# An MoE after three dense layers on one Trainium2 core: tokens gathered from three bf16 parts instead of fp32, expert biases from two fp32r matmuls instead of four fp32

## The chip, the cores and the metric

One of the eight cores of one Trainium2 chip. The metric is the device time of one execution in microseconds, the median of several runs.

## The reference

Two blocks follow each other on 256 tokens of width 1024, all in fp32. The first block has two layers: an RG-LRU mixer and a forgetting attention, each followed by a squared-ReLU MLP. The second has a mixer of stick-breaking attention and an HGRN2 recurrence with gates, then LayerNorm and a mixture of 32 experts, of which each token takes four. The change lies in the mixture:

```
logits = xt @ router_w + router_b
top_vals, top_idx = top_k(logits, 4);  gates = softmax(top_vals)
# for each expert e, on the tokens xblk that chose it:
hcat = xblk @ w_up[e] + b_up[e]                     # 1024 -> 2048
x_glu = min(hcat[:, 0::2], 7);  x_lin = clip(hcat[:, 1::2], -7, 7)
act = x_glu * sigmoid(1.702 * x_glu) * (x_lin + 1)  # 1024
y = act @ w_down[e] + b_down[e]                     # 1024 -> 1024
out = sum over the four experts of gate * y
# then layer_norm(2**0.25 * h + out)
```

## The kernel before

**Dense part (to about 825 us).** Dense weights come in pieces of 1 MiB into the five sections of `area`; ScalarE rounds each half to fp32r (`wh`, line 407), VectorE subtracts the rest (`wl`, line 385), and three fp32r matmuls (lines 487 to 489) make the product. The last one, with `w_out_2`, ends in `residual` for two halves of the tokens and of the columns. Its LayerNorm's statistics come from `bn_stats`; `cross` turns x into `xs` for the router's `logits` (line 1587), `best` and `chosen` find each token's four experts as ones in `M`, and the matmuls `prk` (1654 to 1656) number the tokens of each expert. The order of all instructions is written by hand: each engine runs its own in the order of the code.

**Experts.** A loop goes over 32 positions. `rank_experts` sorts the experts by their load, apart from the first two, so that expert number and column of a position come from the selector `Q`. A position works on one unit of 64 token slots, position 12 on two. For each unit:

- `P` (`spread`, line 1611): 256 tokens x 64 slots of ones and zeros on VectorE, from the position's column. `gather` (1677) multiplies the normed tokens with it on TensorE, line 1685, 8 blocks of 128 columns x 2 halves of the tokens, and VectorE applies the norm's gain and bias (1691, 1692): `xT`, the unit's tokens with columns on the partitions. Columns are taken at every second place, since the weights lie with two rows on one partition.
- `first_layer` (1710): `first_bias` (1547) starts both PSUM banks `hp` with the bias row of the expert: the bias is spread over 4 x 32 partitions in `bup`, and the selector column picks the row. Then 8 weight chunks of 1 MiB with 4 fp32 matmuls each (line 1719); the outputs for gate and linear columns lie in the two halves of the PSUM partitions.
- `gated` (lines 1733 to 1743) on VectorE and ScalarE, while TensorE turns the gates (`pG`, 1704) and gathers the next position's tokens; then TensorE turns the result (`turned`, `paT`, 1761), and ScalarE copies it to `aT`.
- `second_layer`: 4 chunks, 4 fp32 matmuls each (1783); `keep` splits y in two fp32r parts; `combine` (1805, 1806) scatters them into x during the next position.

A matmul of fp32 leaves two records in the trace, of fp32r or bf16 one.

**Weights.** 32 experts x 12 chunks x 1 MiB = 384 MiB come through SyncE's queue into 20 slots of 1 MiB, most in pairs of 2 MiB (`load_chunk`, issued on line 324). `release(j)` after chunk j's last matmul issues the next load into the slots that came free; the functions that `later` names for a place run there too: in position 0 `rank_experts`, `gates_of_tokens`, `number_experts`, `by_token` (which fills `RGT`), `by_position` (`RP`), `residual_sum`, and in position 3 `list_overflow`. The first 20 chunks are loaded during the last dense products, each as soon as a pool closes.

Of the kernel before, what the change touches and what calls it, by code (L numbers as in the profile page):

```python
# [21 lines left out]
KT = 8  # L22
# [56 lines left out]
def shape_constants():  # L79
# [19 lines left out]
    block = i[:, None] // NE == np.arange(4)  # L99
    f["block"] = block  # L100
    f["first"] = (block[:, :, None] & (i[:, None, None] % NE == np.arange(2))).reshape(128, 8)
# [23 lines left out]
def fused(ctx: ExitStack, tc: tile.TileContext, d, out, dbg=None):  # L125
# [1071 lines left out]
    with ExitStack() as mixo, ExitStack() as attn:  # L1197
# [283 lines left out]
        fill((8, rawD))  # L1481
        route_b = mo.tile([128, 2, 128], BF, name="route_b")
# [45 lines left out]
        out_proj(w, [(i, i) for i in range(4)], True)  # L1528
        w = row_weights(d["w_out_2"][0], 512, 512)
# [25 lines left out]
        first_b = C("first").rearrange("p (b e) -> p b e", b=4)  # L1555
        nx = mo.tile([128, 2, D], F32, name="nx")
        xs = [nx[:, t].rearrange("p (k t) -> p k t", k=KT) for t in range(2)]
# [71 lines left out]
        rawF = ctx.enter_context(tc.tile_pool(name="rawF", bufs=1, side="right", reuse_waits="tile"))  # L1629
        fill((14, rawC), (17, rawF))  # L1630
# [20 lines left out]
        early_hps = [[[bank("hp") for _ in range(2)]] for _ in range(2)]  # L1651
        first_bias(early_hps[0], first_b[:, :, 0:1])
# [16 lines left out]
    Q = ml.tile([128, 4, NE], F32, name="Q")  # L1669
# [7 lines left out]
    def gather(P, xT, quick=False):  # L1677

        nxp = nx.rearrange("t a (m p j) -> t a m j p", m=4, j=2)
        gcol, bcol = [V[:, VROWS[n]:VROWS[n] + KT, None].to_broadcast([128, KT, SLOTS]) for n in ("ln1_gp", "ln1_bp")]  # L1680
        for s in (slice(0, 2), slice(2, 5), slice(5, 8)) if quick else (slice(0, KT),):
            p = mm("pX").rearrange("p (k s) -> p k s", k=KT)
            for k in range(s.start, s.stop):
                for t in range(2):
                    pe.matmul(p[:, k], nxp[:, t, k // 2, k % 2], P[:, t], start=(k == s.start and t == 0),  # L1685
                              stop=(k == s.stop - 1 and t == 1), skip_group_check=True)
            if s.stop == 2:
                for k in range(2):
                    act.activation(xT[:, k], p[:, k], AF.Identity, scale=vc("ln1_gp", k), bias=vc("ln1_bp", k))
                continue  # L1690
            dve.tensor_mul(xT[:, s], p[:, s], gcol[:, s])
# [74 lines left out]
    def second_layer(xls, chunks, release, banks=None, fill=None, behind=None):  # L1766
        psum = bank if banks else mm
        aT = turned(xls, psum)
        if fill:
            fill()  # L1770
# [37 lines left out]
    def rank_experts():  # L1808

        pc = mm("pcnt").rearrange("p (a e) -> p a e", e=NE)  # L1810
# [13 lines left out]
        rk4 = wk.tile([128, 4], F32, name="rk4", bufs=1)  # L1824
        dve.scalar_tensor_tensor(rk4, rk.to_broadcast([128, 4]), 1.0, C("block"), op0=OP.add, op1=OP.mult)
        dve.tensor_tensor(Q, C("ranks")[:, None, :].to_broadcast([128, 4, NE]),
                          rk4[:, :, None].to_broadcast([128, 4, NE]), op=OP.is_equal)

    def number_experts():
        pid = mm("pid")  # L1830
        pe.matmul(pid[:1, :NE], C("idcol", 32), Q[:32, 0], start=True, stop=True)
# [9 lines left out]
    def by_position():  # L1841
        prp = mm("prp").rearrange("p (n t e) -> p n t e", n=8, t=2)
        for n in range(2):
            for t in range(2):
                pe.matmul(prp[:, n, t], RGT[:32, n, t * 128:(t + 1) * 128], Q[:32, 0], start=(n + t == 0), stop=True,
# [16 lines left out]
    def residual_sum():  # L1862

        for c in range(2):
# [5 lines left out]
            for t in range(2):  # L1870
                dve.scalar_tensor_tensor(x[:, t, s], nx[:, t, s], ALPHA, gain, op0=OP.mult, op1=OP.mult)
# [9 lines left out]
    def list_overflow():  # L1881
# [6 lines left out]
        for h in range(2):  # L1888
            s = slice(h * NE, (h + 1) * NE)
            pe.matmul(pcp[:1, s], cnt[:32], Q[:32, 0], start=(h == 0), stop=True, skip_group_check=True)  # L1890
# [24 lines left out]
    def spread_units(pos):  # L1915
        for no, j in us_of[pos]:
            ready[no] = {"P": wk.tile([128, 2, SLOTS], F32, name="P")}
# [5 lines left out]
    def gather_units(pos):  # L1923
        for no, _ in us_of[pos]:
            ready[no]["xT"] = wk.tile([128, KT, SLOTS], F32, name="xT")
            gather(ready[no]["P"], ready[no]["xT"], pos == 0)

    def turn_gates(no, psum):
# [6 lines left out]
    gather_units(0)  # L1935
# [15 lines left out]
    }  # L1951

    def expert(pos, middle=None, fill=None):
# [16 lines left out]
        hps = [[bank("hp") for _ in range(2)] for _ in units] if pos > 1 else early_hps[pos]  # L1970
        sel = Q[:, :, pos:pos + 1] if pos > 1 else None
        first_layer(hps, [ready[no]["xT"] for no, _ in units], sel, chunks, release)
# [157 lines left out]
```

## Time and profile before

| | |
|---|---|
| time, median of 3 runs | 1830.05 us (1829.79 to 1831.74) |
| the profiled execution | 1830.76 us, span 1829.0 us |
| TensorE busy | 1768.7 us, 97% |
| VectorE, ScalarE, GpSimd busy | 911.6, 509.7, 67.7 us |
| DMA | 537.96 MB, 294 GB/s on the mean |
| mean granted TensorE clock | 0.986 |
| chain that ended last | PE 89%, DVE 6%, ACT 3% |

A busy share is one of the whole span. The dense part and the experts have different limits, so the stretches of the experts are read apart; what an engine waited for stands behind the bar or in brackets. Granted clock 1.00 is 2.4 GHz, 0.50 is 1.2 GHz.

### The profile page before, as it was taken

To read this page: it belongs to the slowest core of one execution; us is meant where nothing else is said; L and a number is where in the kernel's file an instruction comes from. 1 tells how busy PE (TensorE), PEld (TensorE's weight loads), DVE (VectorE), ACT (ScalarE), POOL (GpSimd) and SP (SyncE) were. 2 spreads that over 40 slices of the span, in tenths; PEclk is the share of its full clock that TensorE was granted. 3 is DMA by queue.
4 is the path that set the end of the run, shared out by engine and by line. 5 is a ranking of instruction groups with operands and counts; after the bars stand their busy time and mean duration, and the time that the engine had idled before them with its cause. 6 is when DMAs were issued, how large, how long until landed. Compare 5 with 4: busy or idle time off the path is not lost.

```text
span 1829.0 us, 27058 instructions
## 1 busy us (share of the span) xinstructions
PE 1768.7 (97%) x11237; PEld 1197.0 (65%) x11237; DVE 911.6 (50%) x1610; ACT 509.7 (28%) x785; POOL 67.7 (4%) x87
## 2 busy tenths in 40 slices
PE   8999999999999999999989999999999999999996
PEld 8899998889999999984343434444443444444342
DVE  7776668768666677663342333323332333323334
ACT  6644445555444455541000001001100001010011
POOL 4020000001000011110000000000000000000000
PEclk9999999999999999999989999999999999999998
DMA  8465553424555544677999999986999999999991
GB/s 268 137 236 185 185 185 121 134 93 158 185 185 187 189 159 134 258 289 294 396 390 378 427 424 427 426 353 244 417 424 427 427 426 426 425 426 426 426 422 49
DMA packets 94366, 537.96 MB, mean 294 GB/s; under 512 B 7088, under 2 KB 20560, under 8 KB 67232
## 3 DMA queue, kind: packets, MB, share of 16 engines
q1 hardware_dynamic: 93360, 534.16, 74.2%
q0 software_dynamic: 736, 1.96, 0.4%
q8 instruction: 90, 1.47, 0.3%
q14 instruction: 36, 0.29, 0.0%
q10 hardware_dynamic: 144, 0.07, 0.0%
HBM read 535.12 MB, written 1.05 MB: 293 GB/s over the span
## 4 chain that ended last, share of the span: by engine, by line
PE 89%; DVE 6%; ACT 3%; issue 1%; POOL 1%; DMA 0%; SPq 0%; ACTq 0%; DVEq 0%; POOLq 0%
PE hp L1719 25%; PE py L1783 13%; PE pX L1685 7%; PE pf L487 5%; PE pf L489 5%; PE pf L488 5%; PE a L489 4%; PE a L487 4%; PE a L488 4%; PE hp L1552 3%; PE pC L1805 2%; DVE wl L385 1%; PE a L844 1%; PE paT L1761 1%; PE pS L1066 1%
## 5 line engine op out<-in xcount | busy, mean ns | idle before, releaser
L385 DVE TENSOR_TENSOR wl<-area,wh 128x1024 fp32r<-128x1024 f32 (+1 forms) x235 | 285.3, 1232 | 141.7 <-ACT wh L407 139.9
L1719 PE MATMUL hp<-raw,xT 128*64 128x512 f32 x1576 | 352.7, 596 | 0.0
L407 ACT CAST wh<-area 128x1024 fp32r<-128x1024 f32 (+1 forms) x238 | 242.3, 1039 | 173.1 <-PE pf L488 94.3
L489 PE MATMUL pf<-hH,wl 128*128 128x256 f32 x928 | 260.0, 280 | 7.5 <-DVE wl L385 7.5
L487 PE MATMUL pf<-hH,wh 128*128 128x256 f32 x928 | 262.2, 283 | 0.1
L488 PE MATMUL pf<-hL,wh 128*128 128x256 f32 x928 | 259.1, 279 | 0.0
L1719 PEld LDWEIGHTS hp<-raw,xT 128*64 128x64 f32 x1576 | 111.0, 137 | 219.0 <-issue 215.6
L1783 PE MATMUL py<-raw,aT 128*64 128x512 f32 x800 | 179.9, 599 | 8.8 <-ACT aT L1763 8.8
L489 PEld LDWEIGHTS pf<-hH,wl 128*128 128x128 f32 x928 | 174.2, 188 | 9.3 <-DVE wl L385 9.3
L1806 DVE TENSOR_TENSOR x<-x,pC 128x512 f32<-128x512 f32 x128 | 79.3, 682 | 197.5 <-PE pC L1805 197.5
L1796 DVE SCALAR_TENSOR_TENSOR y<-py,gcol,y 64x512 fp32r<-64x512 f32 x66 | 49.5, 750 | 256.5 <-ACT y L1795 256.4
L487 PEld LDWEIGHTS pf<-hH,wh 128*128 128x128 f32 x928 | 174.4, 188 | 0.8 <-ACT wh L407 0.6
L488 PEld LDWEIGHTS pf<-hL,wh 128*128 128x128 f32 x928 | 174.0, 188 | 0.1
L1734 ACT ACTIVATE sgm<-sgm 128x256 f32<-128x256 f32 x66 | 27.5, 417 | 497.5 <-DVE sgm L1733 497.5
L489 PE MATMUL a<-aH,wl 128*128 128x256 f32 x512 | 145.0, 283 | 0.0
L487 PE MATMUL a<-aH,wh 128*128 128x256 f32 x512 | 144.9, 283 | 0.0
L488 PE MATMUL a<-aL,wh 128*128 128x256 f32 x512 | 144.9, 283 | 0.0
L1685 PE MATMUL pX<-P,nx 128*128 128x64 f32 x1056 | 133.8, 288 | 0.7 <-DVE M L1660 0.7
L1685 PEld LDWEIGHTS pX<-P,nx 128*128 128x128 f32 x1056 | 132.6, 204 | 0.8 <-issue 0.8
L1783 PEld LDWEIGHTS py<-raw,aT 128*64 128x64 f32 x800 | 55.9, 138 | 117.6 <-issue 102.5
L1719 PE MATMUL hp<-area,xT 128*64 128x512 f32 x536 | 124.1, 602 | 0.0
L1795 ACT ACTIVATE y<-py,gcol 64x512 fp32r<-64x512 f32 x66 | 45.1, 683 | 261.8 <-issue 209.8
(482 smaller groups left out, 2310.5 us busy)
## 6 DMA issues: line engine op xcount, KB each, us to landing
raw<-in_expert_w_up_dram SPq DMA_DIRECT2D x89, 2048.0 KB, 13.7
raw<-in_expert_w_down_dram SPq DMA_DIRECT2D x45, 2048.0 KB, 13.3
area<-in_mlp_w_dram SPq DMA_DIRECT2D x64, 1024.0 KB, 5.3
area<-in_expert_w_up_dram SPq DMA_DIRECT2D x26, 2048.0 KB, 13.6
area<-in_expert_w_down_dram SPq DMA_DIRECT2D x12, 2048.0 KB, 13.3
area<-in_w_in_dram SPq DMA_DIRECT2D x22, 1024.0 KB, 5.2
area<-in_expert_w_up_dram SPq DMA_DIRECT2D x13, 1024.0 KB, 12.6
raw<-in_expert_w_up_dram SPq DMA_DIRECT2D x13, 1024.0 KB, 13.4
```

What stands on the lines that cost most here:

```text
L385: e.tensor_sub(wl, src, wh)
L407: act.copy(wh[:, q], src[:, q])
L487: pe.matmul(out_ap, lh, rh, start=first, stop=False, skip_group_check=True)
L488: pe.matmul(out_ap, lh, rl, start=False, stop=False, skip_group_check=True)
L489: pe.matmul(out_ap, ll, rh, start=False, stop=last, skip_group_check=True)
L1552: pe.matmul(hp[b][64 * g:64 * g + 64], sel[:, 2 * g + b].to_broadcast([128, SLOTS]), bup, start=True, stop=False, skip_group_check=True)
L1685: pe.matmul(p[:, k], nxp[:, t, k // 2, k % 2], P[:, t], start=(k == s.start and t == 0), stop=(k == s.stop - 1 and t == 1), skip_group_che ...
L1719: pe.matmul(hp[b][64 * g:64 * g + 64], xT[:, k], w[:, c0:c0 + 512], start=False, stop=(k == KT - 1), skip_group_check=True)
L1783: pe.matmul(py[c], aT[:, j, g * 64:(g + 1) * 64], w[:, i * D + c * 512:i * D + c * 512 + 512], start=(kt == 0), stop=(kt == KT - 1), skip_ ...
L1795: act.activation(y[0:64, s], py[c], AF.Copy, scale=gcol[h])
L1796: dve.scalar_tensor_tensor(y[64:128, s], py[c], gcol[h], y[0:64, s].bitcast(F32), op0=OP.mult, op1=OP.subtract)
L1806: dve.tensor_add(x[:, t, s], x[:, t, s], p)
```

## The change

- **Gather.** The normed tokens now overwrite x; `nx` is gone. The first unit is gathered in fp32 from x (`first_gather`), its last three column blocks only after the second weight chunk. `three_parts`, called twice in position 0, writes x as three bf16 parts (high, middle, low) into `n3`, which takes the place of `nx` and of the first load of the bias. All other units are gathered by 6 x 8 = 48 bf16 matmuls in place of 16 fp32 ones; `P` is bf16, and xT is finished in two halves of two operations.
- **Bias.** The bias lies as 4 x 32 rows of 1024, rounded to fp32r, and in the second 64 partitions the difference. `first_bias` is two fp32r matmuls over 128 columns: the slots twice, for gate and linear columns. The selector column is copied to 128 slots beforehand (`select`, after the turn of the position ahead); the first position's comes from a constant.
- **Moved.** The bias loads, the load of chunk 17 (behind the end of the dense pools), the copy in `M4`, `rank_experts` and `number_experts` (later in position 0), and the second position's bias, which stood in position 0.

```diff
-        bup = mb.tile([128, 512], F32, name="bup")
-        for g in range(4):
-            sp.dma_start(bup[32 * g:32 * g + 32], d["expert_b_up_2"][0][:, g * 512:(g + 1) * 512])
+        bup = mb.tile([128, D], F32R, name="bup")
...
+        n3 = mo.tile([128, 3, 2, D], BF, name="n3")
+        n3f = n3.rearrange("p i t c -> p (i t c)").bitcast(F32)
+        bias = n3f[:, 2 * D:]
+        for g in range(4):
+            sp.dma_start(bias[32 * g:32 * g + 32], d["expert_b_up_2"][0][:, g % 2 * D:g % 2 * D + D])
...
         out_proj(w, [(i, i) for i in range(4)], True)
+        act.copy(bup, bias)
+        dve.tensor_sub(bup[64:128], bias[64:128], bup[64:128].bitcast(F32))
         w = row_weights(d["w_out_2"][0], 512, 512)
...
                 for b in range(2):
-                    for g in range(2):
-                        pe.matmul(hp[b][64 * g:64 * g + 64], sel[:, 2 * g + b].to_broadcast([128, SLOTS]), bup,
-                                  start=True, stop=False, skip_group_check=True)
+                    pe.matmul(hp[b], sel, bup[:, b * 512:b * 512 + 512], start=True,
+                              stop=False, skip_group_check=True)
...
-                act.activation(nx[:, t, h], x[:, t, h], AF.Identity, scale=rn[t], bias=nm[t])
+                act.activation(x[:, t, h], x[:, t, h], AF.Identity, scale=rn[t], bias=nm[t])
+        act.copy(first_sel, C("first")[:, :, None].to_broadcast([128, 2, SLOTS]))
...
-        dve.tensor_copy(M4[:, :, 1:4], M[:, :, None, :].to_broadcast([128, 2, 3, NE]))
     dense.close()
+    rawF = ctx.enter_context(tc.tile_pool(name="rawF", bufs=1, side="right", reuse_waits="tile"))
+    fill((17, rawF))
...
+    def three_parts(t):
+
+        for c in range(2):
+            s = slice(c * 512, (c + 1) * 512)
+            r = wk.tile([128, 512], F32, name="r", tag=("xl", "sgm")[c], bufs=1)
+            hi, mid, lo = [n3[:, i, t, s] for i in range(3)]
+            act.copy(hi, x[:, t, s])
+            dve.tensor_sub(r, x[:, t, s], hi)
+            act.copy(mid, r)
+            dve.tensor_sub(lo, r, mid)
+
+    def gather(P, xT):
+
+        n3p = n3.rearrange("t i a (m p j) -> t i a m j p", m=4, j=2)
+        p = mm("pX").rearrange("p (k s) -> p k s", k=KT)
+        for i, t in ((0, 0), (1, 0), (0, 1), (1, 1), (2, 0), (2, 1)):
+            for k in range(KT):
+                pe.matmul(p[:, k], n3p[:, i, t, k // 2, k % 2], P[:, t],
+                          start=(i + k + t == 0), stop=(i == 2 and t == 1), skip_group_check=True)
+        for s in (slice(0, 4), slice(4, 8)):
             dve.tensor_mul(xT[:, s], p[:, s], gcol[:, s])
             dve.tensor_add(xT[:, s], xT[:, s], bcol[:, s])
...
     later = {
-        (0, 0): [rank_experts],
-        (0, 1): [gates_of_tokens],
-        (0, 2): [number_experts],
-        (0, 3): [by_token],
+        (0, 1): [lambda: first_gather(P0, ready[0]["xT"], (slice(5, 8),)), rank_experts],
+        (0, 2): [gates_of_tokens, number_experts, lambda: three_parts(0)],
+        (0, 3): [by_token, lambda: three_parts(1)],
         (0, 4): [by_position],
         (0, 5): [residual_sum],
-        (0, 7): [lambda: first_bias(early_hps[1], first_b[:, :, 1:2])],
...
+    def select(q):
+
+        sel = wk.tile([128, 2, SLOTS], F32R, name="sel", tag="xl", bufs=1)
+        dve.tensor_copy(sel, q.bitcast(F32).to_broadcast([128, 2, SLOTS]))
+        return sel.rearrange("p g s -> p (g s)")
```

Two places where the order of the instructions moves (names are tiles, out<-in; a line belongs to the kernel whose piece it is).

VectorE in the last dense product (`wl` is the low part of the weights, `bup` the expert bias; `n_8550` is `n3`):

```order
L1487 TENSOR_SCALAR cd<-ident 128x128
L385 TENSOR_TENSOR wl<-area,wh 128x1024 x4
L1496 TENSOR_TENSOR rw_8559<-rwr,V 128x256 x2
L1498 TENSOR_REDUCE rsum<-rw_8559 128x64
L1575 BN_STATS st<-a 128x6
```

The same with the change:

```order
L1490 TENSOR_SCALAR cd<-ident 128x128
L385 TENSOR_TENSOR wl<-area,wh 128x1024 x3
L1533 TENSOR_TENSOR bup<-n_8550,bup 64x1024
L385 TENSOR_TENSOR wl<-area,wh 128x1024
L1499 TENSOR_TENSOR rw_8560<-rwr,V 128x256 x2
L1501 TENSOR_REDUCE rsum<-rw_8560 128x64
```

The subtraction for the bias now stands ahead of the last low part; on ScalarE the copy to `bup` stands likewise ahead of the last `wh`.

TensorE in an ordinary position before, from the end of one first layer to the next:

```order
L1704 MATMUL pG<-ident,G 128x128 x2
L1685 MATMUL pX<-P,nx 128x64 x16
L1761 MATMUL paT<-ident,xl 128x128 x4
L1783 MATMUL py<-area,aT 64x512 x8
L1783 MATMUL py<-raw,aT 64x512 x8
L1552 MATMUL hp<-bup,Q 64x512 x4
```

And with the change, the end of the gather in position 0, its second layer and position 1's start (`pbd` is the start of the output sum, in position 0 alone):

```order
L1716 LDWEIGHTS n_8550
L1716 MATMUL pX<-P,n_8550 128x64
L1789 MATMUL paT<-ident,xl 128x128 x4
L1813 MATMUL py<-raw,aT 64x512 x16
L1909 MATMUL pbd<-rows,RGT 128x512 x4
L1556 MATMUL hp<-bup,sel 128x512 x2
L1747 MATMUL hp<-area,xT 64x512 x8
```

Of the first two rows 48 pairs stand one after the other. Order and place are as before; the gather is longer in instructions, and the bias shorter.

## Rows read from the trace of the kernel before

**Rows 1.** The page, its parts 1 and 2: the span in 40 equal slices of 45.7 us; TensorE's busy share in tenths, and what the DMA engines moved.
```profile
PE   8999999999999999999989999999999999999996
...
GB/s 268 137 236 185 185 185 121 134 93 158 185 185 187 189 159 134 258 289 294 396 390 378 427 424 427 426 353 244 417 424 427 427 426 426 425 426 426 426 422 49
```

**Rows 2.** The table of stretches, from the last weights of the first position to the last weight's landing and parts of it. Columns: stretch, length, busy us (instructions) of PE, PEld, DVE, ACT, POOL, granted TensorE clock, DMA share, GB/s.
```profile
862.50:1786.30 923.80, 901.34 (x4566) 394.44 (x4564) 308.39 (x668) 89.62 (x188) 0.00 (x0) 0.99 0.97 406
...
940.00:964.00 24.00, 18.51 (x82) 10.94 (x80) 13.53 (x26) 1.48 (x4) 0.00 (x0) 0.72 0.71 299
...
1200.00:1260.00 60.00, 56.28 (x266) 22.66 (x262) 15.13 (x35) 5.69 (x12) 0.00 (x0) 0.94 0.61 232
1260.00:1786.30 526.30, 517.67 (x2656) 225.93 (x2654) 175.90 (x384) 52.62 (x110) 0.00 (x0) 1.00 1.00 424
```

**Rows 3.** The page, part 5, the groups of instructions of the whole execution: busy us, mean ns of one, idle us before them and what ended it.
```profile
L1719 PE MATMUL hp<-raw,xT 128*64 128x512 f32 x1576 | 352.7, 596 | 0.0
...
L1783 PE MATMUL py<-raw,aT 128*64 128x512 f32 x800 | 179.9, 599 | 8.8 <-ACT aT L1763 8.8
...
L1806 DVE TENSOR_TENSOR x<-x,pC 128x512 f32<-128x512 f32 x128 | 79.3, 682 | 197.5 <-PE pC L1805 197.5
```

**Rows 4.** SyncE's queue of DMA issues in order of time, near the end (start us, length us; x2 are two issues, the second at the end of the length).
```profile
1750.01 3.77 SPq L324 DMA_DIRECT2D raw<-in_expert_w_up_dram  x2
```

**Rows 5.** DMA issues of two short stretches (800.0 to 800.3 us, 1753 to 1754 us): KB each, median us from issue to landing.
```profile
raw<-in_expert_w_down_dram SPq DMA_DIRECT2D x1, 2048.0 KB, 8.2
...
raw<-in_expert_w_up_dram SPq DMA_DIRECT2D x1, 2048.0 KB, 22.8
```

**Rows 6.** TensorE in order of time in the last position: chunks 5, 6 and 7 of the first layer, eight records each.
```profile
1795.75 5.32 PE L1719 MATMUL hp<-raw,xT 128*64 128x512 f32 x24
```

**Rows 7.** All engines in order of time, positions 17 and 18 (start us, length us, engine, line, operation, tiles, shapes, records): end of one position and the next.
```profile
1399.75 0.20 PEld L1783 LDWEIGHTS py<-area,aT 128*64 128x64 f32 x4 [0.65 <-ACT aT L1763]
...
1406.67 1.89 PE L1552 MATMUL hp<-bup,Q 128*64 128x512 f32 x8
...
1408.39 1.89 PE L1719 MATMUL hp<-area,xT 128*64 128x512 f32 x8
...
1418.68 0.28 DVE L1611 TENSOR_TENSOR P<-cf,RP 128x128 f32<-128x128 f32 x1
...
1423.78 3.88 PE L1685 MATMUL pX<-P,nx 128*128 128x64 f32 x32
...
1425.51 0.43 DVE L1743 SCALAR_TENSOR_TENSOR xl<-xl,sgm 128x256 f32<-128x256 f32 x1
...
1427.49 0.68 PE L1761 MATMUL paT<-ident,xl 128*128 128x128 f32 x4
...
1428.63 3.65 PE L1783 MATMUL py<-raw,aT 128*64 128x512 f32 x16 [0.46 <-ACT aT L1763]
```

**Rows 8.** TensorE in order of time in the last dense product, fp32r matmuls of 128x512, one a row.
```profile
812.82 0.39 PE L487 MATMUL a<-wh,mH 128*128 128x512 f32 x1
813.05 0.40 PE L488 MATMUL a<-wl,mH 128*128 128x512 f32 x1
```

**Rows 9.** TensorE in order of time, two short stretches: bf16 matmuls in the forgetting attention and in the ranks of the router. Each has its own 128x128 bf16 load, which PEld holds.
```profile
309.14 0.22 PE L1068 MATMUL pS<-ck,cq 96*128 96x128 bf16 x1
309.20 0.22 PE L1070 MATMUL pS<-cb 128*128 128x128 bf16 x1
...
825.47 0.18 PE L1654 MATMUL prk<-M,route_b 128*128 128x32 bf16 x1 [0.30 <-DVE M L1607]
825.49 0.18 PE L1655 MATMUL prk<-M,route_b 128*128 128x32 bf16 x1
825.52 0.18 PE L1656 MATMUL prk<-M,route_b 128*128 128x32 bf16 x1
```

**Rows 10.** All engines in order of time, end of position 3's first layer, and TensorE at the same place of position 12.
```profile
949.52 0.69 PE L1704 MATMUL pG<-ident,G 128*128 128x128 f32 x2 [5.03 <-DVE G L1697]
...
950.00 7.00 PE L1685 MATMUL pX<-P,nx 128*128 128x64 f32 x32
...
952.53 0.43 DVE L1743 SCALAR_TENSOR_TENSOR xl<-xl,sgm 128x256 f32<-128x256 f32 x1
...
956.79 1.06 PE L1761 MATMUL paT<-ident,xl 128*128 128x128 f32 x4
...
1235.96 5.17 PE L1685 MATMUL pX<-P,nx 128*128 128x64 f32 x32
1240.92 1.06 PE L1761 MATMUL paT<-ident,xl 128*128 128x128 f32 x4
```

**Rows 11.** SyncE's issues, ScalarE and VectorE in order of time, from the last dense product to the first gather.
```profile
800.20 0.35 SPq L324 DMA_DIRECT2D raw<-in_expert_w_down_dram  x1
...
803.20 1.05 ACT L407 CAST wh<-area 128x1024 fp32r<-128x1024 f32 x1 [0.16 <-PE a L489]
...
800.67 4.84 DVE L385 TENSOR_TENSOR wl<-area,wh 128x1024 fp32r<-128x1024 f32 x4
...
829.27 0.36 DVE L1691 TENSOR_TENSOR xT<-pX,V 128x192 f32<-128x192 f32 x1 [2.87 <-PE pX L1685]
```

**Rows 12.** The table of stretches again, columns as above: the start of the experts, and position 3's gather.
```profile
828.50:835.30 6.80, 6.80 (x24) 3.88 (x23) 1.43 (x4) 1.10 (x1) 0.00 (x0) 0.50 0.37 152
948.00:961.60 13.60, 11.62 (x46) 8.90 (x48) 6.72 (x17) 1.48 (x4) 0.00 (x0) 0.50 0.65 272
```

More of the change, by code (lines that the diff above doesn't have):

```diff
@@ L1650, in fused @@
         pb = ctx.enter_context(tc.tile_pool(name="pb", bufs=4, space=PSUM, reuse_waits="tile"))
-        early_hps = [[[bank("hp") for _ in range(2)]] for _ in range(2)]
-        first_bias(early_hps[0], first_b[:, :, 0:1])
+        early_hps = [[bank("hp") for _ in range(2)]]
+        first_bias(early_hps, first_sel.rearrange("p b s -> p (b s)"))
         pr = mm("prk").rearrange("p (a e) -> p a e", e=NE)
@@ L1675, in fused, with first_gather @@
     wk = ctx.enter_context(tc.tile_pool(name="moewk", bufs=2, reuse_waits="tile"))
[L1677 to L1681, printed above, removed]
+    gcol, bcol = [V[:, VROWS[n]:VROWS[n] + KT, None].to_broadcast([128, KT, SLOTS]) for n in ("ln1_gp", "ln1_bp")]
+    def first_gather(P, xT, of):
+        xp = x.rearrange("t a (m p j) -> t a m j p", m=4, j=2)
+        for s in of:
             p = mm("pX").rearrange("p (k s) -> p k s", k=KT)
@@ L1684, in gather @@
                 for t in range(2):
-                    pe.matmul(p[:, k], nxp[:, t, k // 2, k % 2], P[:, t], start=(k == s.start and t == 0),
+                    pe.matmul(p[:, k], xp[:, t, k // 2, k % 2], P[:, t], start=(k == s.start and t == 0),
                               stop=(k == s.stop - 1 and t == 1), skip_group_check=True)
@@ L1764, in turned, with second_layer @@
         return aT
-    def second_layer(xls, chunks, release, banks=None, fill=None, behind=None):
+    def second_layer(xls, chunks, release, banks=None, fill=None, behind=None, after=None):
         psum = bank if banks else mm
         aT = turned(xls, psum)
+        if after:
+            after()
         if fill:
@@ L1823, in rank_experts @@
         dve.tensor_scalar(tmp32, krow, kcol, 0.0, op0=OP.is_gt, op1=OP.add, accum_out=rk)
[L1824 to L1827, printed above, removed]
+        rk2 = wk.tile([128, 2], F32, name="rk2", bufs=1)
+        dve.scalar_tensor_tensor(rk2, rk.to_broadcast([128, 2]), 1.0, C("block"), op0=OP.add, op1=OP.mult)
+        dve.tensor_tensor(Q, C("ranks")[:, None, :].to_broadcast([128, 2, NE]),
+                          rk2[:, :, None].to_broadcast([128, 2, NE]), op=OP.is_equal)
     def number_experts():
         pid = mm("pid")
-        pe.matmul(pid[:1, :NE], C("idcol", 32), Q[:32, 0], start=True, stop=True)
+        pe.matmul(pid[:1, :NE], C("idcol", 32), Q[:32, 0].bitcast(F32), start=True, stop=True)
         dve.tensor_copy(ids, pid[:1, :NE])
@@ L1844, in by_position @@
             for t in range(2):
-                pe.matmul(prp[:, n, t], RGT[:32, n, t * 128:(t + 1) * 128], Q[:32, 0], start=(n + t == 0), stop=True,
+                pe.matmul(prp[:, n, t], RGT[:32, n, t * 128:(t + 1) * 128], Q[:32, 0].bitcast(F32), start=(n + t == 0), stop=True,
                           skip_group_check=True)
@@ L1889, in list_overflow @@
             s = slice(h * NE, (h + 1) * NE)
-            pe.matmul(pcp[:1, s], cnt[:32], Q[:32, 0], start=(h == 0), stop=True, skip_group_check=True)
+            pe.matmul(pcp[:1, s], cnt[:32], Q[:32, 0].bitcast(F32), start=(h == 0), stop=True, skip_group_check=True)
         dve.tensor_tensor(ov, pcp[:1, :2 * NE], C("caps", 1), op=OP.is_gt)
@@ L1925, in gather_units @@
             ready[no]["xT"] = wk.tile([128, KT, SLOTS], F32, name="xT")
-            gather(ready[no]["P"], ready[no]["xT"], pos == 0)
+            gather(ready[no]["P"], ready[no]["xT"])
     def turn_gates(no, psum):
@@ L1934, in fused @@
     ready[0] = {"P": P0}
-    gather_units(0)
+    ready[0]["xT"] = wk.tile([128, KT, SLOTS], F32, name="xT")
+    first_gather(P0, ready[0]["xT"], (slice(0, 2), slice(2, 5)))
     rows = wk.tile([128, D], F32, name="rows", tag="y", bufs=1)
@@ L1968, in chunks @@
             return chunk_of.pop((pos, j))
-        hps = [[bank("hp") for _ in range(2)] for _ in units] if pos > 1 else early_hps[pos]
-        sel = Q[:, :, pos:pos + 1] if pos > 1 else None
-        first_layer(hps, [ready[no]["xT"] for no, _ in units], sel, chunks, release)
+        hps = [[bank("hp") for _ in range(2)] for _ in units] if pos else early_hps
+        first_layer(hps, [ready[no]["xT"] for no, _ in units], sels.pop() if pos else None, chunks, release)
         xls = [gated(hps[0])]
@@ L1992, in expert @@
             py = second_layer(xls[n], kept, None if more else release, py, fill,
-                              (lambda: xls.append(gated(hps[n + 1], True))) if more else None)
+                              (lambda: xls.append(gated(hps[n + 1], True))) if more else None,
+                              None if more or pos == NE - 1 else
+                              lambda: sels.append(select(Q[:, :, pos + 1:pos + 2])))
             if waiting:
@@ L2097, in chunks @@
                 return chunk_of["over", k]
-            first_layer([hp], [xT], sc, chunks, lambda k: None)
+            first_layer([hp], [xT], select(Q[:, :, ds(place, 1)]), chunks, lambda k: None)
             py = second_layer(gated(hp), chunks, None)
```

26 lines of the change are left out of this document (13 added, 13 removed).

## The prediction

> **What bounds the kernel now.** I read four views: the page for the stages, the table of stretches for what the DMA engines reach, the order in time of one expert, and the issues of the weight loads.
>
> The page [rows 1] shows TensorE busy in nearly every slice, and from the twentieth on the DMA engines too, at 422 to 427 GB/s. Both can't decide at once; the table says which one does. From 862.5 to 1786.3 us, when the last weight has landed, the loads run at 406 GB/s on the mean, but at 424 with a share of 1.00 from 1260 on [rows 2]; the difference was lost round 950 and 1230, where the share is 0.71 and 0.61. TensorE waits for no weight in that time: the first layer's matmuls have 0.0 us of idle before them, and the second layer's wait only for ScalarE's copies [rows 3]. So **TensorE sets the end today**, with weights in hand: chunk 6 of the last expert was issued at about 1753.5 (second of two issues in 3.77 us from 1750.01), took 22.8 us, so landed near 1776.2, and was used at 1797.5, after a third of the three chunks from 1795.75 [rows 4 to 6].
>
> But the margin is small. One ordinary position takes 28.9 us (second layer at 1399.75, next at 1428.63 [rows 7]); its 12 MiB at 424 GB/s take 29.7 us. A faster TensorE soon meets the loads. The forecast needs both times, and takes the later.
>
> **Bias.** Four fp32 matmuls become two of fp32r. Start to start the old ones cost 1408.39 - 1406.67 = 1.72 us [rows 7]. An fp32r matmul of 128x512 starts 0.23 us after the one before [rows 8], so two take 0.47. Saved: 1.25 us for each of 32 units (positions 1 to 31, position 12 with two), **40.0 us**. `select`, a cast of 128x128, is priced at the 0.28 us of the equally large `P` [rows 7]; VectorE does it a second layer (7 us) ahead of its use and is busy a third of the time (175.90 of 526.30 us [rows 2]), so nothing.
>
> **Gather.** 16 fp32 matmuls (32 records) run from 1423.78 until the turn `paT` at 1427.49: 3.71 us [rows 7]. Now 48 pairs of bf16 load and 64-column matmul. No row has this shape. From below: pairs of 32 columns start 25 ns apart (825.47, 825.49, 825.52); next, a bf16 pair of 128 columns takes 60 ns (309.14 to 309.20); from above, a gather record with its fp32 load takes 3.88/32 = 121 ns [rows 7, 9]. On the line between the first two, 64 columns give 37 ns, and 48 pairs 1.8 us. I take that, because type and load are the same; the ends are 1.2 and 5.8 us.
>
> What is late next is VectorE: the last product of the gating starts 1425.51 and lasts 0.43, so `paT` can't start before 1425.94, 2.16 us after the gather, whatever the gather costs up to 45 ns a pair. With 0.1 us for the hand-over an ordinary gather saves 3.71 - 2.26 = 1.45 us. Twenty-eight positions are such (0 to 30 without 3, 11, 12): 40.6 us. Position 3, where the list of overflows holds VectorE, gathers at the half clock, from 950.00 to 956.79; the product there is ready at 952.96, so 3.8 us. Position 12 gathers at 1235.96 to 1240.92, with its products ready by then: 4.96 - 1.9, 3.1 us [rows 10]. Position 11 gathers twice in 3.6 us, longer than the gating, so saves 1.9 on each: 3.8. Gathers: **51.3 us**. That xT is made in quarters (four operations for two) lies under the second layer.
>
> **The start.** Four things are added there. (a) The two parts of the bias: their load stands behind 2 MiB issued at 800.20 that take 8.2 us [rows 5, 11], so lands near 809.6 (0.5 MiB more at 424 GB/s); ScalarE's copy (1.05) and VectorE's subtraction (at most 1.22) now stand ahead of the last `wh` and `wl`, which then are ready near 811.7 and 813.1; TensorE wants them at 812.82 and 813.05 [rows 8, 11]. About 0.5 us. (b) The selector waits for the four norms, and the two bias matmuls, which were done by then, now stand ahead of the ranks at 825.47 [rows 9]: 0.5. (c) `M4`'s copy now comes after a product and a sum of 0.36 each [rows 11]: some 0.9 us in which the counting waits. (d) `three_parts`: eight subtractions of 128x512 at 0.68 [rows 3], and as many copies on ScalarE; the copy of `RGT` is queued behind four of those copies and two subtractions on ScalarE, by my estimate 1.4 us late for TensorE, and `RP` behind all subtractions, still ahead of the next `P`. Chunk 17's load moves behind the end of the dense pools, a position ahead of its use, and SP has nothing to issue behind it before position 0 releases chunk 1: nothing. Sum 3.3, taken as **3 us**, ends 0 and 6 (the clock is at half from 828.5 to 835.3 already [rows 12], and TensorE now has less to do ahead of that).
>
> **Sum.** TensorE's way: 1829.0 - 40.0 - 51.3 + 3 = 1740.7. The weights' way: the 923.8 us from 862.5 carry 375.1 MB, which at 424 GB/s take 884.6; the 39.2 us of lost time can all go: a position then takes TensorE 28.9 - 2.7 = 26.2 us and the loads 29.7, so issued loads pile up by some 3.5 us a position and bridge the pauses round 950 and 1230. The last weight lands at 1747.1, chunk 6 of the last expert 10.0 before, and from its use TensorE needs 1829.0 - 1797.5 = 31.5 us: 1768.6, and 1 us for that part of the late start that delays the first releases: 1769.6. The later of the two holds, so of 88 us that TensorE saves about 59 arrive. The profiled execution took 1830.76 with a span of 1829.0; 1.8 on top gives **1771 us**. (Its time is 0.7 over the median of 1830.05.)
>
> At the pair's price a rule stands against a row. The row: three pairs, each with a 128x128 bf16 load, start 25 ns apart [rows 9], and the sum by the line through it is the 1771 above. The rule: the Trainium skill, TensorE: Matmul & The Clock Gate, section LDWEIGHTS (loading the stationary operand), lets a load take its columns at 1.2 GHz, 107 ns here, so 5.1 us a gather; by it (an estimate from that page) 28 positions lose 1.4 us each and the end is near 1835. The trace disagrees for contiguous columns; no run here shows bf16 columns read at every second place, as `n3` is. As a mechanism of this kernel that is rival (2).
>
> **Rivals.** (1) *TensorE stays the bound in part.* The pairs take 60 to 80 ns. At 80 the gather is 3.84 us, and ordinary positions gain nothing: saved 40 + 2.9 (position 3) + 1.1 (position 12) - 3 = 41, so 1788 + 2 = 1790; at 60 (2.9 us) TensorE's way is 1764, the lost 39.2 us come back only in part, and the end is near 1777. For: every second column. Against: the line through two rows. The Trainium skill, TensorE: Matmul & The Clock Gate, section Back-to-back issue gap, gives small matmuls some 62 ns each where the hardware decode is off, which would be this case; the trace shows less, but only three in a run.
>
> (2) *Slower: bf16 loads at the pace of fp32 loads.* 121 ns a pair, 5.8 us: an ordinary gather loses 2.1 us, 28 of them 58.8, position 11 4.2, position 12 0.8, position 3 gains 1.0; with 40 won and 3 lost, 1829.0 + 25.8 + 1.8 = 1857 (sum of the losses less the gain: 62.8). It turns from gain to loss near 105 ns a pair, 5.0 us. For: the stride of the columns. Against: [rows 9].
>
> (3) *The starved TensorE loses its clock.* Its way is 29 us the shorter, at 3.5 us a position, so in about the last eight positions it must wait, some 1.4 us for each 2 MiB (4.95 to load; 3.5 to use, since three chunks take 5.32 us [rows 6]). The clock was at 0.50 from 948.0 after TensorE had been idle for 5.03 us [rows 10, 12]. If it falls near the end, the last 12 us of matmuls double: 1783, and up to 1800 if that repeats. Against: between those waits first-layer matmuls run dense, and the bf16 gather is denser than the old.
>
> (4) *The loads run faster than 424 GB/s*, and TensorE's way holds: 1743. Against: 424 with a share of 1.00 [rows 2], and no slice over 427 [rows 1].
>
> **How the numbers follow.** Chances: the forecast 0.61 (1762 to 1777), (1) 0.17 (1777 to 1792), (3) 0.12 (1776 to 1800), (2) 0.07 (1826 to 1857), (4) 0.03. The range 1760 to 1798 takes the forecast, (1) and nearly all of (3). A measurement of this kernel tells about 0.2%, 3.7 us. Rival (2) gives slower 0.06 and, near its turning point, no change 0.02; all else is faster: 0.92.
>
> **What would show it.** Right: `hp` bias records two a unit; gather from first record to `paT` near 2.2 us, `paT` waiting for VectorE's `xl`; DMA share 1.00 from about 880 to the last landing near 1748, without the dip at 1230; and, new, idle before first-layer matmuls ended by DMA in the last eight positions. Wrong: pairs above 45 ns; a last landing later than 1755; no wait for weights at all; clock rows of 0.50 in the last quarter; position 0 more than 6 us longer.

## The result

The change takes 1778.02 us (median of 4 runs, 1777.81 to 1779.86) against 1830.76 of the kernel before (four runs): ratio 0.9714, 95% interval 0.9697 to 0.9731. The profiled execution took 1779.86 with a span of 1778.0. The forecast was 1771, or a span of 1769.6: 8.4 us are to be found in this execution, the slowest of the four, and 7 in the median. A second session gave 1778.54 (1777.0 to 1782.6), ratio 0.9718 [0.9699, 0.9736].

### The profile page after: what moved, and what is told of

Read it like the earlier page. It is cut to its first block, busy times and chain, and to the rows that moved or that the text cites. A ratio compares the mean times of both kernels' runs of the same rounds, so it can differ in the third digit from the quotient of the medians.

```text
span 1778.0 us, 27779 instructions
## 1 busy us (share of the span) xinstructions
PE 1672.7 (94%) x11551; PEld 1112.2 (63%) x11551; DVE 927.3 (52%) x1714; ACT 514.9 (29%) x795; POOL 67.6 (4%) x87
## 4 chain that ended last, share of the span: by engine, by line
PE 66%; DMA 18%; DVE 9%; ACT 3%; issue 1%; POOL 1%; SPq 0%; ACTq 0%; DVEq 0%; POOLq 0%
PE hp L1747 16%; PE py L1813 8%; DMA raw<-in_expert_w_up_dram 8%; DMA area<-in_expert_w_up_dram 6%; PE pf L489 6%; PE pf L487 6%; PE pf L488 5%; DMA raw<-in_expert_w_down_dram 4%; PE a L487 4%; PE a L489 4%; PE a L488 4%; DVE wl L385 1%; PE pC L1835 1%; PE a L844 1%; PE paT L1789 1%
## 5 line engine op out<-in xcount | busy, mean ns | idle before, releaser
L1747 PE MATMUL hp<-raw,xT 128*64 128x512 f32 x1576 | 357.2, 600 | 15.9 <-DMA raw<-in_expert_w_up_dram 15.4
L1761 DVE TENSOR_SCALAR sgm<-hp 128x256 f32<-128x256 f32 x66 | 27.7, 419 | 138.5 <-PE hp L1747 138.5
L487 PEld LDWEIGHTS a<-aH,wh 128*128 128x128 f32 x512 | 98.3, 192 | 0.0
```

The source lines that it names most:

```text
L487: pe.matmul(out_ap, lh, rh, start=first, stop=False, skip_group_check=True)
L1747: pe.matmul(hp[b][64 * g:64 * g + 64], xT[:, k], w[:, c0:c0 + 512], start=False, stop=(k == KT - 1), skip_group_check=True)
L1761: dve.tensor_scalar_min(sgm[b], hv[b][:, :, 0], 7.0)
```

## The profile after

The page of the change, parts 1 and 2, in 40 slices of 44.5 us [rows 1]:

```profile
PE   8999999989999999999998999999999999888885
...
GB/s 275 119 241 189 183 179 140 117 130 127 178 184 189 181 155 141 179 284 299 319 425 426 425 425 426 427 425 424 425 427 426 426 424 426 426 426 426 424 427 215
```

The two rows have changed places: the loads now run at 424 to 427 GB/s in every slice from the twenty-first to the last but one, without a dip, and TensorE shows gaps in the last six. Two stretches of the change [rows 2]: length, busy us of PE, PEld, DVE, ACT, POOL, granted clock, DMA share, GB/s.

```profile
862.50:900.00 37.50, 35.92 (x190) 13.62 (x192) 14.61 (x35) 3.50 (x8) 0.00 (x0) 0.95 0.90 365
900.00:1755.30 855.30, 794.83 (x4792) 304.76 (x4790) 310.98 (x748) 89.55 (x187) 0.00 (x0) 1.00 1.00 424
```

The last weight lands at 1755.30. Up to 900 us the loads are not yet saturated. What TensorE waited for from 900 to 1760 us (us in total, times, the longest):

```profile
PE paT L1789 <- DVE xl L1771: 18.6, 28, 1.2
PE py L1813 <- ACT aT L1791: 15.5, 30, 2.1
PE hp L1747 <- DMA raw<-in_expert_w_up_dram: 15.4, 14, 1.5
PE pG L1732 <- DVE G L1725: 6.2, 2, 5.0
PE hp L1747 <- DMA area<-in_expert_w_up_dram: 3.7, 3, 1.2
```

Third and fifth are new: before, the first layer waited for no weight [rows 3]. All lie from position 23 on. One position's end in the order of time [rows 7]:

```profile
1404.79 1.56 PE L1716 MATMUL pX<-P,n 128*128 128x64 bf16 x48
...
1406.53 0.42 DVE L1771 SCALAR_TENSOR_TENSOR xl<-xl,sgm 128x256 f32<-128x256 f32 x1
1407.01 0.75 PE L1789 MATMUL paT<-ident,xl 128*128 128x128 f32 x4 [0.66 <-DVE xl L1771]
...
1409.12 0.22 DVE L1988 CAST sel<-Q 128x128 fp32r<-128x128 f32 x1
1409.99 5.32 PE L1813 MATMUL py<-raw,aT 128*64 128x512 f32 x24
1415.24 0.72 PE L1556 MATMUL hp<-bup,sel 128*128 128x512 f32 x2
1415.89 0.65 PE L1747 MATMUL hp<-raw,xT 128*64 128x512 f32 x2
```

48 pairs take 1.56 us, under 33 ns each, and the turn `paT` starts 2.22 us after the gather, held by VectorE's `xl`. The bias takes 0.65 us. And the start, TensorE alone, from the first bias to the middle of position 0:

```profile
827.82 1.22 PE L1556 MATMUL hp<-bup,first_sel 128*128 128x512 f32 x2 [2.07 <-ACT first_sel L1648]
...
841.77 0.20 PE L1845 MATMUL pcnt<-route_b,M 128*128 128x1 bf16 x2 [0.93 <-DVE M L1840]
...
849.67 1.07 PE L1876 MATMUL prp<-Q,RGT 32*128 32x32 f32 x8 [1.41 <-ACT RGT L1870]
...
850.67 3.60 PE L1747 MATMUL hp<-raw,xT 128*64 128x512 f32 x8
```

The table of stretches for the last of these rows:

```profile
850.60:854.10 3.50, 3.50 (x10) 0.79 (x9) 2.13 (x4) 1.76 (x3) 0.00 (x0) 0.51 0.54 229
```

Three waits that were terms (b) to (d) of the start, and behind the last a stretch at half the clock (eight records in 3.60 us in place of 1.94) that the forecast did not have.

## The experiments

Theory A, formed after the result: from about 900 us on the loads set the end; TensorE has some 24 us to spare over the rest (the first expectations still say 28), and what delays the releases ahead of 900 us is paid in full. Its rivals are that TensorE still sets the end (D), that the two savings simply share the gain (B), and that TensorE's start no longer counts once the loads bind (E).

**The gather undone.**

```diff
-                pe.matmul(p[:, k], n3p[:, i, t, k // 2, k % 2], P[:, t],
+                pe.matmul(p[:, k], nxp[:, t, k // 2, k % 2], P[:, t], ...
```

> The change with its gather undone: every unit is gathered in fp32 again (a copy of the normed x takes the place of the three bf16 parts), the new bias stays. Theory A (from about 900 us on the loads at 424 GB/s set the end of the change, and TensorE's own way is some 28 us shorter than what was measured): without the gather's saving TensorE's way is 1829 less 32 x 1.07 us for the bias plus some 2 us of start, near 1797, longer than the loads', so 1796 to 1801 us. Rival B (no common limit, the two savings share the 52 us in proportion to their terms of 40 and 51): 1778 + 29 = 1807.

Measured: 1805.58 us, ratio 0.9846 [0.9821, 0.9870], span 1803.7. By the time it lies nearer to B, and A's number was too low; the time alone does not part the two. The trace says why: a position takes 27.97 us, so the bias saves 0.91 us and not the 1.07 that A took; with that, and position 1 starting 4.3 us later than before, 1829 - 32 x 0.91 + 4.3 is 1804. TensorE waits for no weight at all in this kernel (its list from 900 to 1790 us holds `aT`, `G`, and 3.1 us of `xl`, `x` and `y`), as A says; B says nothing on waits.

**The bias undone.**

```diff
-                    pe.matmul(hp[b], sel, bup[:, b * 512:b * 512 + 512], ...
+                    for g in range(2):
+                        pe.matmul(hp[b][64 * g:64 * g + 64], sel[:, 2 * g + b]..., bup, ...
```

> The change with its bias undone: four fp32 matmuls a unit again, no selector, the gather stays in bf16. Theory A: TensorE's way is 1829 less 28 x 1.45, 3.8, 3.8 and 3.1 for the gathers plus 3 to 5 us of start, near 1782, a little longer than the loads' (about 1775), so 1781 to 1786 us: undoing a term of 40 us costs only some 6. Rival B (in proportion): 1778 + 23 = 1801.

Measured: 1787.99 us, ratio 0.9757 [0.9734, 0.9779], span 1783.0: 2 us above A's range and 13 below B, so A, not B. The waits for weights shrink to 2.6 us:

```profile
PE hp L1743 <- DMA raw<-in_expert_w_up_dram: 1.3, 1, 1.3
PE hp L1743 <- DMA area<-in_expert_w_up_dram: 1.3, 1, 1.3
```

The four kernels give a position's length where weights are in hand (start of the first layer of position 14 and of 21, a seventh of the difference):

| | position 14 | position 21 | one position |
|---|---|---|---|
| before | 1292.9 | 1495.0 | 28.88 |
| bias alone (gather undone) | 1282.5 | 1478.3 | 27.97 |
| gather alone (bias undone) | 1267.1 | 1459.2 | 27.45 |
| the change | 1256.7 | 1442.4 | 26.54 |

Bias 0.91, gather 1.43, together 2.34: in TensorE's time the two add up. In the runs, 27 us (bias) and 44 us (gather), each alone, make 53 together, each against the kernel before of its own session.

**TensorE's own way, first attempt.**

```diff
+            part = w // 2 if not isinstance(key, int) else w
-            sp.dma_start(r[:, o:o + w], ap.rearrange("p n c -> p (n c)"))
+            sp.dma_start(r[:, o:o + part], ap.rearrange("p n c -> p (n c)")[:, :part])
```

> The change, but from chunk 24 on each weight load brings only the first half of every partition's bytes, so that the weights are not all there; all matmuls stay. It shows TensorE's own way. Theory A: ten positions of 29.4 us go back to the 26.54 us that positions 14 to 21 take, and the last one loses its waits: 1749 to 1754 us, no wait for weights left. Rival C (TensorE's waits are worth only the 19.1 us that the list of waits gives to loads): 1759 to 1761. Rival D (the end is set by TensorE, the waits are incidental): 1775 to 1778.

The condition in this edit never held, so all loads were whole, and the run is a repeat of the change: 1778.66 us (1777.38 to 1785.66). It tells nothing on TensorE's way. Its profiled execution, the longest one, is of use below.

**TensorE's own way.**

```diff
+        half = two and not isinstance(e, int)
...
-            chunk_of[key, j + k] = r[:, k * 2048:(k + 1) * 2048]
+            chunk_of[key, j + k] = r[:, :2048] if half else r[:, k * 2048:(k + 1) * 2048]
```

> The change, but from position 2 on each load of two chunks brings only the first chunk, and the matmuls of the second chunk read the first one's bytes: half of those weights, all matmuls. It shows TensorE's own way with loads out of the way. Theory A: positions 23 to 30, which take 27.3 to 30.6 us, go back to 26.54 (22.9 us), and position 31 loses some 5 us of waits: 1749 to 1754 us, no first-layer wait for weights. Rival C (TensorE's waits are worth only the 19.1 us that the list of waits puts down to loads): 1759 to 1761. Rival D (TensorE sets the end anyway): 1775 to 1779.

Measured: 1756.15 us (1755.99 to 1760.75), ratio 0.9595 [0.9571, 0.9620]. All positions from 13 to 30 take 26.5 us, and no wait for weights is left; the longest waits in its list are:

```profile
PE paT L1790 <- DVE xl L1772: 18.4, 28, 1.2
PE py L1814 <- ACT aT L1792: 15.9, 31, 2.1
PE pG L1733 <- DVE G L1726: 6.2, 2, 5.0
```

From position 1's first layer to the end it takes 878.9 us (1758.6 - 879.7), the change 903.0 (1778.0 - 875.0): the loads cost the change 24 us. The time is 2 us above A's range, whose 5 us for the last position were really 1.4; D is out, and C's 19.1 us fall short of the 24.

**The same kind of delay at two places.**

```diff
-        (0, 1): [lambda: first_gather(P0, ready[0]["xT"], (slice(5, 8),)), rank_experts],
+        (0, 1): [lambda: first_gather(P0, ready[0]["xT"], (slice(5, 8),), 4), rank_experts],
```

> The change with the third part of the first unit's gather made four times over (the first three are overwritten): 3 x 1.63 = 4.9 us more on TensorE, behind chunk 1 of position 0. Theory A (the loads bind from about 900 us on, and what delays the releases ahead of that delays the last landing): last landing and end 4 to 5 us later than in the change, 1782 to 1784. Rival E (the loads bind, TensorE's start does not count): 1778.

```diff
-            gather(ready[no]["P"], ready[no]["xT"])
+            gather(ready[no]["P"], ready[no]["xT"], 5 if pos == 17 else 1)
```

> The change with the gather at the end of position 16 made five times over: 4 x 1.56 = 6.2 us more, less the 0.66 in which the turn waited for VectorE anyway, so 5.6 us more on TensorE, at about 1335 us, with 17 to 20 us of weights in hand. Theory A: the lead shrinks by that, the waits for weights start about two positions earlier, and the end stays: 1777 to 1779. Rival D (each us of TensorE counts wherever it lies): 1783 to 1784.

Measured: 1781.78 us (ratio 0.9736 [0.9708, 0.9763]) in position 0, and 1777.41 (0.9708 [0.9680, 0.9737]) in position 16. There position 16 grew by 6.4 us, from 26.54 to 32.91, and none of it arrived. The waits for weights began at position 25, two positions later than in the change and not earlier, as the expectation had it: while TensorE is held up, the loads go on and get further ahead. In position 0 some 3 us of the 4.9 arrived; position 0 had grown only by 2.3 (43.52 us against 41.19 in the change, once more). The three further gathers took 4.2 us there; the wait at `prp` stayed, but behind it the clock stayed at its upper level, and eight records took 1.94 us (3.12 in the change, once more):

```profile
853.17 1.07 PE L1876 MATMUL prp<-Q,RGT 32*128 32x32 f32 x8 [1.40 <-ACT RGT L1870]
854.17 1.94 PE L1747 MATMUL hp<-raw,xT 128*64 128x512 f32 x8
```

The two intervals overlap; the traces decide, in the table behind the next two.

**The start in another order.**

```diff
+        (0, 0): [copy_M4, lambda: three_parts(0)],
...
-        (0, 2): [gates_of_tokens, number_experts, lambda: three_parts(0)],
+        (0, 2): [gates_of_tokens, number_experts],
```

and `first_sel` is copied ahead of the norms.

> The change with its start put in another order: the selector's copy for the first position ahead of the four norms on ScalarE, the copy into M4 and the first half of the three parts behind chunk 0 (VectorE is idle there for 5.7 us) instead of behind chunks 1 and 2, so that the copy of RGT waits for nothing. Theory A with the start paid in full (the loads are not yet saturated before 900 us, so each us that the first releases come earlier is a us at the end): TensorE saves 0.9 at the selector, 0.9 at pcnt, 1.4 at prp, and perhaps the half clock after it (1.7); 1773 to 1776 us. Rival E (once the loads bind, TensorE's start no longer counts): 1778, no difference.

Measured: 1774.61 us (1771.0 to 1775.85), ratio 0.9676 [0.9656, 0.9697]; all five executions lie below the 13 of the change in three sessions (from 1777.0 up). The waits at `hp`, `pcnt` and `prp` are gone, and so is the half clock behind them:

```profile
825.75 0.71 PE L1556 MATMUL hp<-bup,first_sel 128*128 128x512 f32 x2
...
847.16 1.07 PE L1879 MATMUL prp<-Q,RGT 32*128 32x32 f32 x8
848.16 1.94 PE L1747 MATMUL hp<-raw,xT 128*64 128x512 f32 x8
```

At the selector only 0.7 us are won, since TensorE now waits 1.84 us at the ranks `prk` for VectorE's `M`.

**The bias loaded ahead of chunk 8.**

```diff
-        fill((8, rawD))
         n3 = mo.tile([128, 3, 2, D], BF, name="n3")
...
             sp.dma_start(bias[32 * g:32 * g + 32], ...)
+        fill((8, rawD))
```

> The change with the start in the other order (as in mended), and also the four loads of the bias issued ahead of the 2 MiB of chunk 8 instead of behind them. Theory A (a late landing of those 2 MiB holds ScalarE's copy of the bias, with it the last high and low parts of the weights, and so TensorE; each us of start is paid at the end): the bias lands near 806 us instead of 810.4 to 815.3, the copy waits for it no longer than 2 us, the executions in which the bias lands late are gone; 1770 to 1774 us. Rival G (the late landings come from something else that also delays the rest): the same time as mended, 1774 to 1775.

> The change as it is, once more, beside mended_b on the same chip: 1777 to 1780 us, with single executions up to 1786 where the bias lands late.

Measured: 1775.96 us (1772.2 to 1776.1), ratio 0.9695 [0.9679, 0.9711], the change beside it 1778.54. The mechanism does what A says. ScalarE's copy of the bias and the last `wh` behind it, in the change, in the longest execution of its repeat, and here:

```profile
811.10 1.04 ACT L1532 CAST bup<-n 128x1024 fp32r<-128x1024 f32 x1 [6.45 <-DMA n<-in_expert_b_up_dram]
812.05 1.04 ACT L407 CAST wh<-area 128x1024 fp32r<-128x1024 f32 x1
```

```profile
815.42 1.04 ACT L1533 CAST bup<-n 128x1024 fp32r<-128x1024 f32 x1 [11.00 <-DMA n<-in_expert_b_up_dram]
816.37 1.04 ACT L408 CAST wh<-area 128x1024 fp32r<-128x1024 f32 x1
```

```profile
805.07 1.05 ACT L1532 CAST bup<-n 128x1024 fp32r<-128x1024 f32 x1 [2.56 <-DMA n<-in_expert_b_up_dram]
806.03 1.04 ACT L407 CAST wh<-area 128x1024 fp32r<-128x1024 f32 x1
```

In the second, TensorE's last dense product waits for `wh` and then for `wl`:

```profile
817.46 0.50 PE L488 MATMUL a<-wh,mH 128*128 128x512 f32 x1 [2.06 <-ACT wh L408]
819.03 0.50 PE L489 MATMUL a<-wl,mH 128*128 128x512 f32 x1 [1.07 <-DVE wl L386]
```

But the time lies above A's range, and the median is no better than that of the start in another order (`mended` in the expectation), whose five executions show no long one either (1775.85 at most; its profiled one has no such wait). So the late landing is shown in the profiles of two long executions (the repeat here, and that of the halved bytes, 1760.75 us, where `wh` and `wl` are waited for by 0.82 and 1.06 us); that it makes the other long ones is not shown, nor that loading the bias first is worth anything in the median.

What all of these have in common, from the profiled executions:

| kernel | fp32 product in the last dense stage (`a<-cd,x`) starts | position 1's first layer starts | last weight lands | from position 1 to the landing | span |
|---|---|---|---|---|---|
| the change | 811.01 | 875.04 | 1755.30 | 880.3 | 1778.0 |
| the change, once more | 808.81 | 873.15 | 1753.49 | 880.3 | 1776.3 |
| its repeat with the late bias | 810.96 | 880.85 | 1761.78 | 880.9 | 1783.9 |
| delay in position 0 | 809.93 | 876.67 | 1757.31 | 880.6 | 1780.0 |
| delay in position 16 | 808.90 | 873.18 | 1753.64 | 880.5 | 1776.3 |
| start in another order | 811.15 | 870.66 | 1751.46 | 880.8 | 1774.0 |
| and the bias first | 809.00 | 869.00 | 1747.65 | 878.7 | 1770.3 |
| half a gather (below) | 809.46 | 873.50 | 1756.96 | 883.5 | 1779.5 |
| before | 808.55 | 869.46 | 1786.24 | 916.8 | 1829.0 |

With the change and its variants position 1 starts at times 12 us apart, the loads take 880 to 881 us from there in all but two, and 22 to 23 us behind the last landing the kernel ends. The first column differs by 2.3 us from execution to execution, ahead of all that the experiments move. Counted from there to position 1, the change takes 64.0 and 64.3 us, the delay in position 0 66.7, the start in another order 59.5, and with the bias first 60.0. Theory A holds, E is out.

**Half a gather.**

```diff
-        for i, t in ((0, 0), (1, 0), (0, 1), (1, 1), (2, 0), (2, 1)):
+        for i, t in ((0, 0), (0, 1), (2, 1)):
```

> The change with 24 pairs a gather in place of 48 (half of the products of the three parts left out). Theory A (behind the gather VectorE's last gating product holds the turn): pairs 0.78 us shorter, wait of the turn for VectorE longer by the same, position period 26.54 us as before, time 1778. Rival F (the gather itself is on the way): 25.8 us a position where weights are in hand.

Measured: 1781.46 us (1781.30 and 1781.63), 3 us slower than the change with fewer matmuls, and 3 above what A said. Of the ordinary positions about half take 26.54 us, as A says; the others, mostly every second one, 28.24, which neither theory had. Two neighbouring positions, TensorE, and the stretches behind the first turn and round the second:

```profile
1303.03 0.86 PE L1716 MATMUL pX<-P,n 128*128 128x64 bf16 x24
1305.24 0.75 PE L1789 MATMUL paT<-ident,xl 128*128 128x128 f32 x4 [1.35 <-DVE xl L1771]
1306.45 7.93 PE L1813 MATMUL py<-raw,aT 128*64 128x512 f32 x28 [0.46 <-ACT aT L1791]
...
1333.48 0.75 PE L1789 MATMUL paT<-ident,xl 128*128 128x128 f32 x4 [1.35 <-DVE xl L1771]
1334.69 5.80 PE L1813 MATMUL py<-raw,aT 128*64 128x512 f32 x26 [0.46 <-ACT aT L1791]
```

```profile
1306.90:1310.40 3.50, 3.50 (x12) 1.02 (x10) 0.64 (x3) 0.00 (x0) 0.00 (x0) 0.51 1.02 435
1330.90:1338.00 7.10, 5.29 (x48) 2.77 (x48) 4.59 (x14) 1.35 (x4) 0.00 (x0) 1.00 1.00 427
```

The turn waits 1.35 us in place of 0.66, and behind mostly every second such wait the granted clock is 0.51 for 3.5 us, which costs 1.7. The 3 us at the end are lost by the loads (883.5 us from position 1 to the landing). TensorE releases later here, and where little is in hand the loads run out of slots:

```profile
940.00:964.00 24.00, 16.99 (x90) 6.49 (x86) 13.80 (x29) 1.48 (x4) 0.00 (x0) 0.79 0.94 384
1200.00:1260.00 60.00, 54.16 (x292) 20.20 (x288) 23.47 (x59) 7.17 (x16) 0.00 (x0) 1.00 0.99 414
```

In the change these stretches ran at 421 and 425 GB/s; the difference is 3.6 us of loading. That TensorE's delay is the reason is read from these rows; no run tried it.

## Why the prediction was right, and where not

**The time, by itself.** 1778.02 us lies 1 us past the 1762 to 1777 that the forecast gave to its own mechanism, in the ranges of rivals (1) and (3). Neither of them came; the mechanism is the forecast's, with a sum that is 7 us too low.

**The bound changed sides, as forecast.** TensorE's time fell by far more than arrived, the loads took over at 424 GB/s, and the waits for weights stand in the last nine positions. Shown by the halved bytes (24 us come back) and by the delay in position 16 (6.4 us, none of it arrives).

**Gather: right.** 1.45 us forecast, 1.43 measured. The pair costs less than the 37 ns taken, and that made no difference, since VectorE's `xl` holds the turn (2.22 us against 2.26); half a gather leaves an undisturbed position at 26.54. Rivals (1) and (2) needed 60 and 121 ns. In the kernel with the gather five times over, a load's record lasts 99 ns, but 1632 of them (the whole stretch from 900 to 1740 us) keep PEld busy for 52.9 us, 32 ns each:

```profile
L1716 PEld LDWEIGHTS <-n 128*128 128x128 bf16 x1632 | 52.9, 99 | 1.9 <-issue 1.6
```

So the loads overlap, and columns at every second place cost nothing that shows against the 37 ns of the line; no run has contiguous columns of this shape beside it. The Trainium skill, TensorE: Matmul & The Clock Gate, section LDWEIGHTS (loading the stationary operand), makes such a load 107 ns (an estimate by its formula): near the length of one record, and three times the step from one to the next, which is what a gather is made of. The 62 ns a matmul that the forecast sets beside rival (1) did not come either; that the hardware decode is off in this case, as it supposed, no run shows.

**Bias: mis-sized, 0.91 us for 1.25.** The step "an fp32r matmul of 128x512 starts 0.23 us after the one before" was read in a row of fp32r products that follow each other [rows 8]. Here the pair stands between fp32 matmuls: two take 0.65, the `py` before them starts 0.53 ahead in place of 0.43, and the first chunk's first matmul takes 0.05 more. The kernel before had rows of such a change, in the last dense product: behind fp32 matmuls the second fp32r one starts 0.31 after the first, not 0.23:

```profile
812.04 0.48 PE L487 MATMUL a<-wh,mH 128*128 128x512 f32 x1
812.35 0.39 PE L488 MATMUL a<-wl,mH 128*128 128x512 f32 x1
```

The missing 0.34 a unit is 11 us on TensorE's way, and cost the forecast nothing, because that way no longer sets the end.

**Start: mis-sized, and its weight wrong.** This is one of the two steps that failed. Of the 3 us for TensorE it charged the weights' way with 1, "that part of the late start that delays the first releases". The table above shows that all of it counts. Position 1's first layer started 5.6 us later than before: 2.45 of them were there already at a dense product that the change leaves as it was (808.55 before, 811.01 here; in the other profile of the change 808.81, so this part varies from execution to execution), and 3.1 come from there to the end of position 0, although it had by then saved 1.4 on a gather and 1 on a bias. So the additions cost some 5.5 us, inside the ends of 0 and 6: by their rows, the selector 0.9 (0.5 forecast), the count 0.9 and `prp` 1.4 (as forecast), and the half clock 1.7, which the forecast did not have; the bias's own conversion, forecast at 0.5, shows no wait in this profile. The other order took 4.4 of them away (position 1 at 870.66).

**"The 39.2 us of lost time can all go": not the part ahead of 900 us.** This is the other step that failed. From 862.5 to 900 the loads ran at 365 GB/s, which against 424 loses 5.2 us, about as before. Loads can pile up only behind releases, and here each load was issued as soon as its slot was free: from 862 to 900 us SyncE's issues wait for TensorE alone (34.4 us), for no earlier load. The forecast let the surplus begin at 862.5.

**The sum again.** Last landing 1747.1 forecast, 1755.30 measured. 5.2 us are the slow stretch; at 862.5 there was more left to load (37.5 us at 365 GB/s and 855.3 at 424, 376.3 MB for 375.1), some 3 us at 424, uncertain by 1 or 2 for GB/s in whole numbers, which is the late start: 8 for the measured 8.2. Behind the landing 22.7 us for 21.5; less the 1 us that was charged, that is the 8.4. Some 2 of these are the late dense product of this execution: in the change, once more, the span was 1776.3. The forecast's own bound, a last landing later than 1755, was just passed, and pointed at this.

**Rivals (3) and (4)** did not come: the granted clock was 1.00 through the starved positions, with waits of up to 1.5 us between dense first-layer matmuls, and the pace was 424. Half a gather shows that (3) was no idle fear: there the clock fell at the turn, where several waits and short matmuls follow each other.

## What to carry to other kernels

Where two resources are nearly equal, forecast both ways to the end and ask from which moment the second is saturated: work saved behind that moment is lost above the difference, and work added ahead of it is paid in full, whichever engine does it. Look for the price of an operation in a row with the same neighbours, not only of the same shape. And place one-time work (conversions, constants) where its engine idles, in front of nobody's queue: the start in another order is the faster kernel, 1774.6 us for 1778.

## What the runs showed of the hardware

- Less work made TensorE slower: with 24 pairs in place of 48 the wait at the turn grew from 0.66 to 1.35 us and the granted clock fell to 0.51 for 3.5 us behind mostly every second one. The Trainium skill, TensorE: Matmul & The Clock Gate, section HAM oscillation — how this bites in real kernels, tells of waits for DMA that do this to every burst; here the fall came behind a wait for VectorE, and in the change waits for DMA of up to 1.5 us brought none (granted clock 1.00 from 900 to 1755 us).
- One core drew 424 GB/s over 855 us; near the end a 2 MiB load took some 4.9 us of that. The Trainium skill, Perfetto Trace Analysis, section Roofline, has about 435 GB/s as the bound of the 16 DMA engines of a core that is alone; the trace agrees, 424 being 97% of it.
- With the loads saturated, SyncE issued them late: the last piece (0.5 MiB) at 1730.58, 21 us after the matmuls that had used its slot, by the order of the chunks, ended near 1709.5. The list of its waits from 900 to 1760 us puts 297 us, in 82 waits of at most 5.7, down to earlier loads; before, it had none of these. The four lines of that kind are:

```profile
SPq L324 <- DMA raw<-in_expert_w_up_dram: 146.1, 38, 5.7
SPq L324 <- DMA raw<-in_expert_w_down_dram: 72.6, 21, 5.1
SPq L324 <- DMA area<-in_expert_w_up_dram: 56.0, 16, 4.6
SPq L324 <- DMA area<-in_expert_w_down_dram: 22.3, 7, 4.4
```

The DMA share stayed at 1.00, so no cost shows; what in an earlier load holds the issue was not tried.
